# Another spacing for the first tile's rows, with the rows left out moved in two parts at the end

## The chip, the cores and the metric

The kernel runs on one core of one Trainium2 chip; nothing else runs beside it. The metric is the device time of one execution in microseconds (us). Lower is better.

## The reference

The kernel divides each row of 1024 values by the sum of the row's absolute values. There are 32 x 512 = 16,384 rows; 67.11 MB are read and as much is written.

```
x = np.random.randn(32, 512, 1024).astype(np.float32)
sums = np.sum(np.abs(x), axis=-1, keepdims=True)
return (x / (sums + 1e-8)).astype(np.float32)
```

## The kernel before

The tiles lie in SBUF, the core's working memory, in 128 partitions; each partition takes 128 of the 16,384 rows. The kernel moves them in eleven tiles: ten of 12 rows per partition (6 MB each) and a last one of 8. Within a tile a partition's rows lie together in DRAM, so neighbouring partitions of a 12-row tile start 12 x 4 KB = 48 KB apart. Loads are issued from the SP queue and stores from the ScalarE queue. Four tiles are in SBUF at a time. VectorE sums the absolute values and multiplies two thirds of the rows; ScalarE multiplies the other third.

```
    R = 12
    BUFS = 4
    per_partition = n // P
    ...
    rows = [R] * (per_partition // R)
    if per_partition % R:
        rows.append(per_partition % R)

    def piece(flat, i):
        a, k = P * sum(rows[:i]), rows[i]
        return flat[a : a + P * k, :].rearrange("(p r) d -> p r d", p=P)
    ...
    def normalize(x_tile, r0, k, kv):
        ...   # reduce of |x|, + EPS, reciprocal; VectorE multiplies kv rows, ScalarE the others

    with tc.manual_schedule():
        for i, k in enumerate(rows):
            x_tile = sbuf.tile([P, R, d], FP32)
            nc.sync.dma_start(out=x_tile[:, :k, :], in_=piece(x_flat, i))
            normalize(x_tile, 0, k, k - k // 3)
            nc.scalar.dma_start(out=piece(out_flat, i), in_=x_tile[:, :k, :])
```

## Time and profile before

| | before |
|---|---|
| time, median of the first 3 runs | 317.24 us (316.94 to 317.64) |
| span of the profiled run | 315.7 us |
| VectorE / ScalarE busy | 75% / 15% |
| DMA engines busy, by slices | 9 tenths in 38 of 40 slices |
| bytes moved, mean rate | 134.23 MB, 425 GB/s |

First some lines of the profile page of the kernel before. The line `DMA` gives the busy share of the 16 DMA engines in 40 equal slices, in tenths, and `GB/s` what they moved in each. The line of a group gives its busy time, the mean of one instruction in ns, and the idle time of the engine ahead of it. A line of the DMA issues ends with the KB of one transfer and the us from issue to landing.

```profile
span 315.7 us, 205 instructions
...
DVE 235.8 (75%) x44; ACT 46.1 (15%) x43; POOL 0.2 (0%) x4
...
DMA  8999999999999999999999999999999999999996
GB/s 318 467 405 436 455 380 423 405 473 423 399 479 417 405 479 411 423 461 411 455 436 405 473 417 405 473 423 399 486 406 411 479 413 421 438 455 411 455 401 274
DMA packets 3169, 134.23 MB, mean 425 GB/s; under 512 B 352, under 2 KB 352, under 8 KB 352
...
HBM read 67.11 MB, written 67.11 MB: 425 GB/s over the span
...
L45 DVE TENSOR_REDUCE s<-x_tile 128x12 f32<-128x12288 f32 (+1 forms) x11 | 138.2, 12562 | 58.0 <-DMA x_tile<-in_x_dram 58.0
...
x_tile<-in_x_dram SPq DMA_DIRECT2D x10, 6144.0 KB, 34.9
out_dram<-x_tile ACTq DMA_DIRECT2D x10, 6144.0 KB, 51.3
...
```

One line of the table of waits of the kernel before (total us, times, longest us):

```profile
...
DVE s L45 <- DMA x_tile<-in_x_dram: 58.0, 8, 18.6
...
```

And the timeline of the kernel before (start, length in us): the first reduce, then the end.

```profile
...
18.63 12.95 DVE L45 TENSOR_REDUCE s<-x_tile 128x12 f32<-128x12288 f32 x1 [18.63 <-DMA x_tile<-in_x_dram]
...
277.61 0.34 ACTq L74 DMA_DIRECT2D out_dram<-x_tile  x1
279.65 8.69 DVE L45 TENSOR_REDUCE s<-x_tile 128x8 f32<-128x8192 f32 x1 [2.13 <-DMA x_tile<-in_x_dram]
...
288.88 6.56 DVE L55 TENSOR_TENSOR x_tile<-x_tile,inv 128x6144 f32<-128x6144 f32 x1
295.53 0.34 ACTq L74 DMA_DIRECT2D out_dram<-x_tile  x1
```

The reader is to see two things. VectorE waits 58.0 us for loads, and its whole work of 235.8 us would fit under the transfers, so the DMA engines are the limit. And near the end VectorE is nowhere late enough to matter: the last store is issued at 295.53 us, while the DMA line is at 9 tenths until the last slice (a slice is 7.9 us).

The trace also records each single DMA packet with its queue, start, length and bytes. In this kernel one packet is one partition's part of a transfer: 49,152 bytes, or 32,768 in the last tile. The records don't name the engine. I joined each packet to the one whose end its start meets within 25 ns, which gives, in the kernel before, 16 chains of 8,388,608 bytes each, one for each engine, with hardly a gap. Two numbers from there carry the argument: the median 48 KB packet takes 1.815 us, and the one of 32 KB 1.213 us. Sixteen engines at 48 KB per 1.815 us are 433 GB/s. The Trainium skill, "DMA: Bandwidth & Descriptors", section "Where 436 GB/s comes from", puts the limit of the SBUF side at 435.2 GB/s; this trace agrees. So all but the edges of the run is at the ceiling.

Times from the packet records are counted from the start of the first packet, which is at 1.73 us on the clock of the timelines. Times with "issued" or "reduce" are from the timelines.

The lengths of the first packet of each of the 16 engines in load 0, from the same records, us, in order of their starts:

```
before  2.79 2.24 3.15 2.50 3.14 2.51 2.64 2.66 3.71 2.38 2.32 3.56 2.18 2.05 1.82 1.86
```

All but the last two are clearly longer than 1.815. This was the only visible slack at the start, and the change aims at it.

### The profile page before, as it was taken

To read this page: it belongs to the slowest core of one execution; us is meant where nothing else is said; L and a number is where in the kernel's file an instruction comes from. 1 tells how busy PE (TensorE), PEld (TensorE's weight loads), DVE (VectorE), ACT (ScalarE), POOL (GpSimd) and SP (SyncE) were. 2 spreads that over 40 slices of the span, in tenths; PEclk is the share of its full clock that TensorE was granted. 3 is DMA by queue.
4 is the path that set the end of the run, shared out by engine and by line. 5 is a ranking of instruction groups with operands and counts; after the bars stand their busy time and mean duration, and the time that the engine had idled before them with its cause. 6 is when DMAs were issued, how large, how long until landed. Compare 5 with 4: busy or idle time off the path is not lost.

```text
span 315.7 us, 205 instructions
## 1 busy us (share of the span) xinstructions
DVE 235.8 (75%) x44; ACT 46.1 (15%) x43; POOL 0.2 (0%) x4
## 2 busy tenths in 40 slices
DVE  0069999999999699739947991997399469979400
ACT  0010501303105003200500050032005000502000
POOL 0000000000000000000000000000000000000000
DMA  8999999999999999999999999999999999999996
GB/s 318 467 405 436 455 380 423 405 473 423 399 479 417 405 479 411 423 461 411 455 436 405 473 417 405 473 423 399 486 406 411 479 413 421 438 455 411 455 401 274
DMA packets 3169, 134.23 MB, mean 425 GB/s; under 512 B 352, under 2 KB 352, under 8 KB 352
## 3 DMA queue, kind: packets, MB, share of 16 engines
q1 hardware_dynamic: 1584, 67.11, 49.7%
q10 hardware_dynamic: 1584, 67.11, 49.1%
q14 instruction: 1, 0.01, 0.0%
HBM read 67.11 MB, written 67.11 MB: 425 GB/s over the span
## 4 chain that ended last, share of the span: by engine, by line
another core or an unknown queue 36%; DMA 31%; DVE 26%; SPq 0%; issue 0%; DVEq 0%; ACTq 0%
DMA x_tile<-in_x_dram 15%; DMA out_dram<-x_tile 15%; DVE s L45 15%; DVE x_tile L55 10%; SPq L72 0%; DVE inv L54 0%; DVE s L52 0%; DVEq L54 0%; ACTq L74 0%
## 5 line engine op out<-in xcount | busy, mean ns | idle before, releaser
L45 DVE TENSOR_REDUCE s<-x_tile 128x12 f32<-128x12288 f32 (+1 forms) x11 | 138.2, 12562 | 58.0 <-DMA x_tile<-in_x_dram 58.0
L55 DVE TENSOR_TENSOR x_tile<-x_tile,inv 128x8192 f32<-128x8192 f32 (+1 forms) x11 | 93.5, 8498 | 0.4
L62 ACT ACTIVATE x_tile<-x_tile,inv 128x1024 f32<-128x1024 f32 x42 | 44.9, 1137 | 226.3 <-DVE inv L54 226.3
L62 ACT ACT_TABLE_LOAD x1 | 1.3, 1283 | 18.7 <-DMA x_tile<-in_x_dram 18.7
L54 DVE RECIPROCAL inv<-s 128x12 f32<-128x12 f32 (+1 forms) x11 | 2.5, 225 | 0.9
L52 DVE TENSOR_SCALAR s<-s 128x12 f32<-128x12 f32 (+1 forms) x11 | 1.9, 173 | 0.4
L89 POOL MEMSET const-bfloat16-1.0<- 128x1 bf16 x1 | 0.1, 101 | 0.0
L89 POOL MEMSET const-uint8-127<- 128x1 uint8 x1 | 0.1, 101 | 0.0
L89 POOL MEMSET const-float32-0.0<- 128x1 f32 x1 | 0.1, 98 | 0.2 <-issue 0.2
L89 POOL MEMSET const-float32-1.0<- 128x1 f32 x1 | 0.1, 98 | 0.0
## 6 DMA issues: line engine op xcount, KB each, us to landing
x_tile<-in_x_dram SPq DMA_DIRECT2D x10, 6144.0 KB, 34.9
out_dram<-x_tile ACTq DMA_DIRECT2D x10, 6144.0 KB, 51.3
x_tile<-in_x_dram SPq DMA_DIRECT2D x1, 4096.0 KB, 30.4
out_dram<-x_tile ACTq DMA_DIRECT2D x1, 4096.0 KB, 19.1
```

Source lines behind the costliest of these rows:

```text
L45: nc.vector.tensor_reduce(out=s[:, :k], in_=x_tile[:, r0 : r0 + k, :], axis=mybir.AxisListType.X, op=mybir.AluOpType.add, apply_absolute_v ...
L52: nc.vector.tensor_scalar_add(out=s[:, :k], in0=s[:, :k], scalar1=EPS)
L54: nc.vector.reciprocal(out=inv[:, :k], in_=s[:, :k])
L55: nc.vector.tensor_mul(out=x_tile[:, r0 : r0 + kv, :], in0=x_tile[:, r0 : r0 + kv, :], in1=inv[:, :kv].unsqueeze(2).to_broadcast([P, kv, d]),)
L62: nc.scalar.activation(out=row, in_=row, func=mybir.ActivationFunctionType.Copy, scale=inv[:, r : r + 1],)
L89: nc = _bacc.Bacc("TRN2", target_bir_lowering=False, num_devices=1)
```

## The change

The intent, read from the diff: have the first tile's partitions start 64 KB apart in DRAM, by taking 12 of every 16 rows. The 4 rows that are left out of every 16 join the last tile. Since those and the 4 rows that remain at the end are not one region of DRAM, the last tile is loaded, normalized and stored in two parts of 4 rows.

```diff
-    rows = [R] * (per_partition // R)
-    if per_partition % R:
-        rows.append(per_partition % R)
+    FIRST = 16
+    rows = [R] * (per_partition // R) + [8]
 
-    def piece(flat, i):
-        a, k = P * sum(rows[:i]), rows[i]
-        return flat[a : a + P * k, :].rearrange("(p r) d -> p r d", p=P)
+    def block(flat, a, k):
+        return flat[P * a : P * (a + k), :].rearrange("(p r) d -> p r d", p=P)
+
+    def pieces(flat, i):
+        head = block(flat, 0, FIRST)
+        if i == 0:
+            return [(0, R, head[:, :R, :])]
+        a = FIRST + R * (i - 1)
+        if i < len(rows) - 1:
+            return [(0, R, block(flat, a, R))]
+        return [
+            (0, FIRST - R, head[:, R:, :]),
+            (FIRST - R, per_partition - a, block(flat, a, per_partition - a)),
+        ]
...
-            nc.sync.dma_start(out=x_tile[:, :k, :], in_=piece(x_flat, i))
-            normalize(x_tile, 0, k, k - k // 3)
-            nc.scalar.dma_start(out=piece(out_flat, i), in_=x_tile[:, :k, :])
+            for r0, m, src in pieces(x_flat, i):
+                nc.sync.dma_start(out=x_tile[:, r0 : r0 + m, :], in_=src)
+            for r0, m, dst in pieces(out_flat, i):
+                normalize(x_tile, r0, m, m - m // 3)
+                nc.scalar.dma_start(out=dst, in_=x_tile[:, r0 : r0 + m, :])
```

More of the change, by code (lines that the diff above doesn't have):

```diff
@@ L28 @@
     BUFS = 4
+    FIRST = 16
     per_partition = n // P
-    assert n % P == 0
-    rows = [R] * (per_partition // R)
-    if per_partition % R:
-        rows.append(per_partition % R)
-    def piece(flat, i):
-        a, k = P * sum(rows[:i]), rows[i]
-        return flat[a : a + P * k, :].rearrange("(p r) d -> p r d", p=P)
+    assert n % P == 0 and per_partition % R == 8
+    rows = [R] * (per_partition // R) + [8]
[12 more added lines that the diff above has]
+        ]
     sbuf = ctx.enter_context(tc.tile_pool(name="sbuf", bufs=BUFS))
@@ L69 @@
     with tc.manual_schedule():
-        for i, k in enumerate(rows):
+        for i in range(len(rows)):
             x_tile = sbuf.tile([P, R, d], FP32)
-            nc.sync.dma_start(out=x_tile[:, :k, :], in_=piece(x_flat, i))
-            normalize(x_tile, 0, k, k - k // 3)
-            nc.scalar.dma_start(out=piece(out_flat, i), in_=x_tile[:, :k, :])
+            for r0, m, src in pieces(x_flat, i):
[3 more added lines that the diff above has]
+                nc.scalar.dma_start(out=dst, in_=x_tile[:, r0 : r0 + m, :])
 _INS = ['x']
```

## The prediction

> **What bounds the kernel now.** DMA, from end to end. The page shows the DMA engines busy at 9 tenths in 38 of 40 slices, 134.23 MB at a mean of 425 GB/s. VectorE is busy 75%, ScalarE 15%; VectorE's largest wait (58.0 us in total, the table of waits) is for loads. The trace's single DMA packets say it more sharply: each of 128 partitions is one packet (48 KB, 32 KB in the last tile), 8 per DMA engine and transfer. The median 48 KB packet takes 1.815 us, the 32 KB one 1.213 us, so an engine's share is 2 x (80 x 1.815 + 8 x 1.213) = 309.8 us. From the first packet's start to the last one's end are 312.6 us. Only 2.8 us is not pure packet time on the engine that ends last.
>
> Where those 2.8 us are: the first packet of each engine takes 1.82 to 3.71 us, and two engines take 3.57 and 3.71. Nothing evens this out, as every engine has the same bytes: two engines, by their phase those two, end at 325.1 and 325.4 on the trace's clock, the others at 324.0 to 324.6. The slowest first packet sets the end.
>
> **What the change does.**
> 1. Start: the first tile's partitions begin 64 KB apart instead of 48 KB. Bytes and packets of load 0 stay; only which addresses the 16 engines hit together changes. If the slow pair becomes like the rest, about 1.0 us is gained; if power-of-two spacing makes more engines collide, 1 or 2 us are lost. The Trainium skill, "DMA: Bandwidth & Descriptors", section "Latency and other measured facts", reports 207 GB/s at a row pitch of 512 KiB against 214 padded, and large losses only from 2 MiB, so I expect no lasting slowdown at 64 KB; this trace has no such pitch to confirm it.
> 2. Tail: the last 8 rows per partition move as two parts of 4. VectorE's work is the same (8.69 + 6.56 us today, twice about 4.35 + 3.3 us after) plus one more set of small operations, 0.5 us. The 16 KB packets should take 0.61 us (from 1.815 and 1.213); 16 more packets per engine at 9 ns are 0.15 us.
> 3. Section "Queues, rings and completion order" of that page says that the engines alternate between queues packet by packet. 16 KB load packets then get a quarter of an engine beside 48 KB store packets, so the second part lands later: I estimate at 294 us, where today the last load's wait ends at 279.65. Its store is issued near 303 us instead of 295.5. But stores 7 to 9 and the first part's store advance by what the loads give up, and should keep the engines busy until about 308. The 4 to 5 us of slack should hide it.
>
> **On the critical path:** the first packets, wholly; of the tail only the 0.15 us.
>
> **Predicted:** 316.9 us, 8 in 10 between 315.8 and 318.6. Faster by over 2%: 0.01; within 2%: 0.96; slower by over 2%: 0.03. A gain of 2% (6.3 us) is ruled out by the 2.8 us above.
>
> **What would show it.** Step 1: the longest first packet of load 0, and the first reduce's start (18.63 us now); right if the end moves with the slowest first packet. Step 2: two 128x4096 reduces near 4.35 us. Step 3: the last reduce starting near 294 us and DMA still 9 tenths in every slice but the last.
>
> **What would make it wrong.** A wait between the parts that I don't foresee (part two's multiply waiting for part one's store, or a semaphore in use), idling the DMA engines by 5 to 10 us; step 3's slack being smaller; 64 KB spacing slowing all 8 packets of load 0.

## The result

| | before | after |
|---|---|---|
| median of 6 runs | 317.30 us (316.94 to 317.74) | 318.17 us (317.69 to 318.61) |
| span of the profiled run | 315.7 us | 316.8 us |
| ratio | | 1.0028, interval 1.0013 to 1.0043 |

A ratio here and below is the mean time of one kernel's fast runs over that of the other's in the same rounds, so not quite the ratio of the medians. The change costs 0.3%: the same within 2%, but measurably slower, where a small gain had been predicted.

The page of the changed kernel, the lines that answer to those of before:

```profile
span 316.8 us, 214 instructions
...
DVE 236.3 (75%) x48; ACT 46.3 (15%) x43; POOL 0.2 (0%) x4
...
DMA  8999999999999999999999999999999999999995
GB/s 323 472 397 478 416 366 428 403 484 403 441 453 397 459 434 397 478 416 416 478 397 459 434 397 465 428 410 484 397 448 447 397 459 420 389 447 472 397 411 250
DMA packets 3458, 134.24 MB, mean 424 GB/s; under 512 B 384, under 2 KB 384, under 8 KB 384
...
HBM read 67.11 MB, written 67.11 MB: 424 GB/s over the span
...
L58 DVE TENSOR_REDUCE s<-x_tile 128x12 f32<-128x12288 f32 (+1 forms) x12 | 138.3, 11527 | 63.6 <-DMA x_tile<-in_x_dram 63.6
...
x_tile<-in_x_dram SPq DMA_DIRECT2D x10, 6144.0 KB, 34.1
out_dram<-x_tile ACTq DMA_DIRECT2D x10, 6144.0 KB, 50.8
x_tile<-in_x_dram SPq DMA_DIRECT2D x2, 2048.0 KB, 34.1
...
```

The table of waits of the changed kernel, one line:

```profile
...
DVE s L58 <- DMA x_tile<-in_x_dram: 63.6, 8, 17.6
...
```

And its timeline, the first reduce and the end:

```profile
...
17.62 12.95 DVE L58 TENSOR_REDUCE s<-x_tile 128x12 f32<-128x12288 f32 x1 [17.62 <-DMA x_tile<-in_x_dram]
...
276.85 4.41 DVE L58 TENSOR_REDUCE s<-x_tile 128x4 f32<-128x4096 f32 x1
...
281.77 3.36 DVE L68 TENSOR_TENSOR x_tile<-x_tile,inv 128x3072 f32<-128x3072 f32 x1
...
285.22 0.34 ACTq L89 DMA_DIRECT2D out_dram<-x_tile  x1
293.40 4.42 DVE L58 TENSOR_REDUCE s<-x_tile 128x4 f32<-128x4096 f32 x1 [8.27 <-DMA x_tile<-in_x_dram]
...
298.75 3.36 DVE L68 TENSOR_TENSOR x_tile<-x_tile,inv 128x3072 f32<-128x3072 f32 x1
302.19 0.34 ACTq L89 DMA_DIRECT2D out_dram<-x_tile  x1
```

What to see: the first reduce starts at 17.62 us instead of 18.63, so load 0 was 1.0 us faster. The two small reduces are there (4.4 us each), the second part's data are waited for until 293.40 us, and its store is issued at 302.19 instead of 295.53. The DMA line is at 9 tenths up to the last slice all the same. So a microsecond was won at the start, no engine was left idle, and yet the end came a microsecond later. The page can't say more than that; the single packets can. (This profiled run took 318.61 us, the slowest of the six, so its trace shows the loss a little larger than the median does.)

First packets of load 0 in the changed kernel, us, in order of their starts:

```
after   2.51 2.60 2.62 2.53 2.39 2.58 2.60 2.45 2.55 2.51 2.65 2.48 2.47 2.25 2.47 2.22
```

The 3.71 and the 3.56 are gone. And the slow packets between 245 and 292 us after the first packet's start, all that took more than 60 ns over the usual length (start, length, kind; `store 48` is a 48 KB packet of a store):

```
before   271.003  1.467 load 32     271.353  1.366 load 32        (usual: 1.213)

after    258.005  1.996 store 48    258.025  2.024 store 48    258.057  2.020 store 48    258.108  1.880 store 48
         260.540  1.885 store 48    260.605  1.880 store 48    260.652  1.908 store 48    260.681  1.936 store 48
         265.466  2.456 store 48    265.519  2.531 store 48    265.554  2.565 store 48    265.625  2.598 store 48
         265.694  2.608 store 48
         285.469  2.007 store 48    285.596  2.021 store 48    285.666  2.074 store 48    285.769  2.111 store 48
         285.849  2.111 store 48                                   (usual: 1.815)
```

They lie on the same five chains, each of which loses 1.0 to 1.5 us there by the lengths of all its packets. Of the 16 engines the middle ones are done at 311.5 us after the first packet's start in both kernels; the last one is done at 312.61 in the kernel before and at 313.84 in the changed one. All engines have the same bytes, so nobody takes over what a slow one has left.

### The profile page after: what moved, and what is told of

Same layout as the page of the kernel before. It is cut to its first block, busy times and chain, and to the rows that moved or that the text cites. A ratio compares the mean times of both kernels' runs of the same rounds, so it can differ in the third digit from the quotient of the medians.

```text
span 316.8 us, 214 instructions
## 1 busy us (share of the span) xinstructions
DVE 236.3 (75%) x48; ACT 46.3 (15%) x43; POOL 0.2 (0%) x4
## 4 chain that ended last, share of the span: by engine, by line
another core or an unknown queue 36%; DMA 35%; DVE 23%; SPq 1%; issue 0%; DVEq 0%; ACTq 0%
DMA x_tile<-in_x_dram 19%; DMA out_dram<-x_tile 16%; DVE s L58 14%; DVE x_tile L68 9%; SPq L86 1%; DVE inv L67 0%; DVE s L65 0%; DVEq L67 0%; ACTq L89 0%
```

## The experiments

Twelve runs were made: eight new kernels, two of them twice, and the two known ones again. The theory after the result (T): the 64 KB start wins about 1 us, and the split tail loses about 2 us. The rivals: R1, the even start leaves the engines in step so that they collide later, and the tail is harmless; R2, the 64 KB spacing of the left-out rows slows the tail, not the split.

### The start alone (two runs of the same kernel)

```diff
-            nc.sync.dma_start(out=x_tile[:, :k, :], in_=piece(x_flat, i))
+            src = piece(x_flat, i)
+            if i == 0:
+                src = x_flat[: P * 16, :].rearrange("(p r) d -> p r d", p=P)[:, :R, :]
+            nc.sync.dma_start(out=x_tile[:, :k, :], in_=src)
```

> The kernel before with one thing changed: load 0 reads 12 of every 16 rows (64 KB apart), everything else as before; the result is wrong on purpose (some rows of tile 0 are others). Theory T (the start gains about 1 us by evening out the first packets; the split tail loses about 2 us again): slowest first packet near 2.6 us instead of 3.7, first reduce near 17.6 us instead of 18.6, all engines end within about 0.7 us of one another, time about 1 us under before (316.3). Rival R1 (the even start itself leaves the engines in step, and they collide later; the tail is harmless): first packets even as well, but slow packets at the first store and in the tail, ends spread over 2 us, time 0.5 to 1 us over before.

Measured: 317.35 us median of 5 runs against 317.26 for before; ratio 1.0000, interval 0.9988 to 1.0013. Its output is wrong, which doesn't matter for the time. The timeline shows the early first reduce:

```profile
...
17.71 12.95 DVE L45 TENSOR_REDUCE s<-x_tile 128x12 f32<-128x12288 f32 x1 [17.71 <-DMA x_tile<-in_x_dram]
...
```

The slowest first packet took 2.63 us, and in the profiled run all engines ended within 0.5 us of one another, with no slow packet in the tail. That run was the fastest of the five (316.58 us). In the mean nothing was gained. So the tail is innocent as long as it is whole, against R1; but T's gain of 1 us does not reach the end either. It was run again later:

> The start alone at 64 KB again (wrong result on purpose), for more times and a second trace. The cold starts showed 0.7 us less per load, so a load-by-load theory says 0.7 us under before (ratio 0.998). W (the end is set by the sum of all delays of the worst engine, and the gain at the first packet is partly paid back at the first store, which then hits all engines in step): ratio between 0.9985 and 1.000; engines' mean end 0.1 to 0.3 us under that of before's traces.

Measured: ratio 0.9999, interval 0.9982 to 1.0016, median 317.56 of 6 runs. Here three 32 KB packets of the last load took 1.9 to 2.0 us instead of 1.2, on three engines, and the last engine ended at 312.94 us after the first packet's start, 1.2 us after the mean. W's first half, the ratio, came as expected; its second, the engines' mean end, was 311.69 against 311.61 and 311.69 in the two traces of before: no gain there.

### The tail alone

The first tile is contiguous as before; the last tile's two parts are two contiguous blocks of 4 rows.

```diff
-        head = block(flat, 0, FIRST)
-        if i == 0:
-            return [(0, R, head[:, :R, :])]
-        a = FIRST + R * (i - 1)
+        a = R * i
...
-            (0, FIRST - R, head[:, R:, :]),
-            (FIRST - R, per_partition - a, block(flat, a, per_partition - a)),
+            (0, 4, block(flat, a, 4)),
+            (4, 4, block(flat, a + 4, 4)),
```

> First tile as before (48 KB apart), only the last 8 rows per partition in two parts of 4, both contiguous. Correct result. T: the tail alone costs about 2 us on some engines: time 1 to 2 us over before (318.3 to 319.3), slow store packets (2.0 to 2.6 us instead of 1.8) while 16 KB load packets run beside them. R1: 0.15 us over before (317.5), no such slow packets. Rival R2 (it is the 64 KB spacing of the left-out rows that slows the tail, not the split): 317.5 as well.

Measured: 318.30 us against 317.26; ratio 1.0034, interval 1.0022 to 1.0047; correct. Nine slow store packets (up to 2.52 us) between 245 and 292 us, and the last engine ends at 313.64. The four engines that hold these nine packets are the four that end last (312.81 to 313.64; all others by 311.99). This is the whole loss of the change, without its start and without its 64 KB spacing. R2 falls, and R1 with it. T's sign is right and its size is nearer to 1 us than to 2.

### Another spacing: 12 of every 20 rows

```diff
-    FIRST = 16
+    FIRST = 20
...
             (0, FIRST - R, head[:, R:, :]),
-            (FIRST - R, per_partition - a, block(flat, a, per_partition - a)),
```

With 80 KB between partitions the left-out rows are 8 per partition, which is the whole last tile, one load and one store.

> First tile takes 12 of every 20 rows (80 KB apart), the 8 rows it leaves out are the last tile, whole, one load and one store with 32 KB packets as before. Correct result. T, if any spacing other than 48 KB evens the start: 1 us under before (316.3). If 64 KB is special: slowest first packet 3 us or more, time within 0.3 us of before or above. R1: near before or 0.5 us above although the first packets are even.

Measured: 317.35 us against 317.26; ratio 1.0004, interval 0.9990 to 1.0018; correct. The slowest first packet took 2.94 us. So 64 KB is hardly special in this one trace, and again an even start gave no time. Five 32 KB packets of the last load were slow (up to 1.81 us instead of 1.21).

### The left-out rows in the second tile (two runs of the same kernel)

```diff
-        a = FIRST + R * (i - 1)
-        if i < len(rows) - 1:
-            return [(0, R, block(flat, a, R))]
-        return [
-            (0, FIRST - R, head[:, R:, :]),
-            (FIRST - R, per_partition - a, block(flat, a, per_partition - a)),
-        ]
+        if i == 1:
+            return [(0, 4, head[:, R:, :]), (4, 8, block(flat, FIRST, 8))]
+        a = R * i
+        return [(0, rows[i], block(flat, a, rows[i]))]
```

This keeps the 64 KB start and the whole last tile. The small load packets now run while no store is under way yet.

> 64 KB start as in the change, but the 4 rows that it leaves out join the second tile (4 + 8 rows in two parts) and the last tile is 8 rows in one part as before. Correct result. T: start gain kept and no split tail: 0.5 to 1 us under before (316.3 to 316.8), first reduce near 17.6 us. R1: ends spread as in the changed kernel, 0.5 to 1 us over before. R2: tile 1's loads have slow packets or its stores have.

Measured: 316.94 us against 317.26; ratio 0.9996, interval 0.9983 to 1.0008; correct. Again for a tighter interval:

> 64 KB start with the left-out rows in the second tile, again, for a tighter interval: within 0.3 us of before, below the changed kernel by about 1 us, no slow store packets between 245 and 292 us.

Measured: 316.94 us against 317.28; ratio 0.9986, interval 0.9970 to 1.0001. The medians are 0.34 us apart, just over the 0.3 expected. Both traces have a single slow store packet after 245 us (2.17 us), not none as expected. The loss of the change is gone in this arrangement: on the same chip, the changed kernel took 318.04 us. Whether it beats the kernel before is not shown: both intervals contain 1.

### Cold starts

Before the real loop, 24 loads into one buffer, each waiting for the one before; spacing 48 KB and 64 KB in turn.

```diff
     with tc.manual_schedule():
+        x_tile = sbuf.tile([P, R, d], FP32)
+        for i in range(24):
+            a, span = 8 * (i // 2), (12, 16)[i % 2]
+            src = x_flat[P * a : P * (a + span), :].rearrange("(p r) d -> p r d", p=P)
+            nc.sync.dma_start(out=x_tile, in_=src[:, :R, :])
+            t = stats.tile([P, R], FP32)
+            nc.vector.tensor_reduce(out=t[:, :1], in_=x_tile[:, :1, :], ...)
         for i, k in enumerate(rows):
```

> Before the real loop, 24 loads of 12 rows per partition into one buffer, each waiting for a small reduce of the one before, so that all DMA engines are idle at each start; even ones with partitions 48 KB apart, odd ones 64 KB apart. Correct result; the time is longer on purpose. S (the spacing evens out the first packets): the slowest first packet of the 12 starts at 64 KB has a mean at least 0.5 us below that of the 12 at 48 KB. D (it is a draw of each execution): the two distributions overlap, means within 0.3 us of each other.

Measured (761.09 us in all, one run), from the packet records, 12 loads each, mean and standard deviation:

```
                                       48 KB apart    64 KB apart
slowest first packet                   3.46 (0.15)    2.75 (0.10) us
mean of the 16 first packets           2.58 (0.06)    2.47 (0.06) us
first packet's start to last one's end 16.38 (0.11)   15.66 (0.08) us
```

S is right: the two spacings took turns within one execution, and the wider one evens out the first packets, and a load into idle engines is 0.72 us shorter. But the second row shows how that comes about: the mean engine gains only 0.11 us. The load ends when its last engine ends, so the load gains 0.7; the engines together gain little.

### Where the loss of the tail sits: stores split, or loads split

Both have the start of the kernel before. In the first the last 8 rows are loaded whole, then normalized and stored in two parts; in the second they are loaded in two parts, then normalized and stored whole. Against the kernel of the tail alone, the two parts are now the halves of the same 8 rows:

```diff
-            (0, 4, block(flat, a, 4)),
-            (4, 4, block(flat, a + 4, 4)),
+            (0, 4, block(flat, a, 8)[:, :4, :]),
+            (4, 4, block(flat, a, 8)[:, 4:, :]),
...  # the first kernel, loads whole:
-            for r0, m, src in pieces(x_flat, i):
+            for r0, m, src in [(0, rows[i], block(x_flat, R * i, rows[i]))]:
...  # the second kernel instead, stores whole:
-            for r0, m, dst in pieces(out_flat, i):
+            for r0, m, dst in [(0, rows[i], block(out_flat, R * i, rows[i]))]:
```

> 48 KB start as before; the last 8 rows are loaded whole (32 KB packets), normalized and stored in two parts of 4 rows. Correct result. If the small load packets are the cause of the tail's loss (L): within 0.3 us of before (317.3). If splitting the compute and the stores is (C): 1 us over before (318.3).

Measured: 317.39 us against 317.35; ratio 0.9998, interval 0.9984 to 1.0011; correct. No slow packet between 245 and 292 us. Its timeline: two reduces again, but the data of both are there at 279.22 us, as before.

```profile
...
279.22 4.42 DVE L55 TENSOR_REDUCE s<-x_tile 128x4 f32<-128x4096 f32 x1 [1.96 <-DMA x_tile<-in_x_dram]
...
287.43 4.41 DVE L55 TENSOR_REDUCE s<-x_tile 128x4 f32<-128x4096 f32 x1
...
296.24 0.34 ACTq L86 DMA_DIRECT2D out_dram<-x_tile  x1
```

> 48 KB start as before; the last 8 rows are loaded in two parts of 4 rows (16 KB packets), normalized and stored whole. Correct result. L: 1 us over before (318.3), with slow store packets (2.0 to 2.6 us) near the end of stores 7 and 8. C: within 0.3 us of before.

Measured: 324.01 us against 317.35; ratio 1.0205, interval 1.0191 to 1.0219; correct. There are 26 slow store packets (up to 2.45 us) between 245 and 292 us, so L holds for the packets. The time was missed by far, for a second reason, which its page and timeline show:

```profile
span 323.0 us, 207 instructions
...
DMA  8999999999999999999999999999999999999547
...
```

```profile
...
277.48 0.34 ACTq L86 DMA_DIRECT2D out_dram<-x_tile  x1
294.82 8.69 DVE L55 TENSOR_REDUCE s<-x_tile 128x8 f32<-128x8192 f32 x1 [17.43 <-DMA x_tile<-in_x_dram]
...
310.69 0.34 ACTq L86 DMA_DIRECT2D out_dram<-x_tile  x1
```

The last reduce waits until 294.82 us, and as it is now one of 8 rows, the store is issued only at 310.69. By then the earlier stores have run out: the packet chains of the engines have holes of 6.3 to 8.5 us, and the DMA line drops to 5, 4 and 7 tenths in the last slices. So splitting the load makes its end later, and only the split of the compute and the store, which the change also makes, keeps that off the end.

Why the load ends later is seen in the packets of one engine of the changed kernel, in order, from 250.2 us on (L load, S store, KB; 0 is the small packet that signals the end of a transfer):

```
S48 L0 S48 L16 S48 L16 S48 L16 S48 L16 S48 L16 S48 L16 S0 L16 S48 L16 S48 L0 S48 L16 S48 ...
```

A load packet and a store packet take turns. The Trainium skill, "DMA: Bandwidth & Descriptors", section "Queues, rings and completion order", says that each engine goes round the queues packet by packet, and the trace agrees. With packets of 16 KB against 48 KB a load gets a quarter of the engine.

### The kernel before, once more

> The kernel before, unchanged, for a second profile. S: again a pair of first packets at 3.5 to 3.7 us and the last engines 1 us behind the rest. D: another slowest first packet (between 2.6 and 3.7 us) on another engine, and the end moves with it.

Measured: one look, 317.06 us. The slowest first packet took 3.74 us, as S says, but the next took 3.04, so there was no pair. And that engine was not alone at the end: three ended within 0.06 us of one another, the last at 312.29 us after the first packet's start, and the next one at 311.90. The two beside it had first packets of 2.16 and 2.22 us which had started 1.1 to 1.2 us late. What the three have in common is that their first packets ended last of all, 3.33 to 3.77 us after the first start.

### The changed kernel, once more

> The changed kernel again, for a second trace beside the others: about 0.9 us over before (ratio 1.003); first packets even (slowest below 3 us), four to six engines with slow store packets in the tail, and the last engine at least 1 us behind the median one.

Measured: 318.04 us against 317.28; ratio 1.0021, interval 1.0004 to 1.0037. The slowest first packet took 2.92 us, and 28 store packets were slow (up to 2.82 us) between 245 and 292 us. Eight of them began within 1.1 us, so at least eight engines had one, not the four to six expected. This trace also has slow load packets at 112, 131, 141, 198 and 231 us, of which the first trace of the same kernel has a single one (at 229 us); they are unexplained, and they delay many engines at once. The last engine ended at 314.18 us, 1.0 us after the mean of all. The profiled run was the slowest of its six (318.83).

### Small load packets in the middle of the run

```diff
-            nc.sync.dma_start(out=x_tile[:, :k, :], in_=piece(x_flat, i))
+            src = piece(x_flat, i)
+            for r0, m in [(0, 4), (4, 8)] if i == 5 else [(0, k)]:
+                nc.sync.dma_start(out=x_tile[:, r0 : r0 + m, :], in_=src[:, r0 : r0 + m, :])
```

> The kernel before with only tile 5's load split into a part of 4 rows (16 KB packets) and one of 8 rows (32 KB), in the middle of the run; everything else as before, correct result. G (small load packets beside 48 KB store packets are slow anywhere): slow store packets (1.9 to 2.6 us) during tile 5's load on some engines, summing to at least 2 us over the engines, time 0.3 to 1 us over before. P (it belongs to the tail): no slow packets there, time within 0.3 us of before.

Measured: 339.35 us against 317.28; ratio 1.0686, interval 1.0663 to 1.0708; correct. Nobody expected that. Its page and the wait for tile 5:

```profile
span 336.8 us, 208 instructions
...
DMA  8999999999999999999999999999999999529747
...
```

```profile
...
155.25 12.95 DVE L45 TENSOR_REDUCE s<-x_tile 128x12 f32<-128x12288 f32 x1 [22.81 <-DMA x_tile<-in_x_dram]
...
```

During tile 5's load 23 store packets were slow, by 3.8 us in sum over the engines, so G is right there. But the load took 44 us (107.1 to 151.3), where tile 5's load takes 28 in the kernel before, as its packets of 16 and 32 KB take turns with store packets of 48 KB; VectorE waited 22.81 us for it, tile 5's store came late, and the later loads stayed late too (VectorE waits 11.13 us ahead of tile 9, against 6.78 in the kernel before). From 180 us on, 161 packets were slow although all but the last load's and store's were 48 KB again, and near the end most engines ran dry ahead of each of the last two stores, which were issued at 303.18 and 324.43 us (a DMA line of 5, 2, 9, 7, 4 and 7 tenths). So packets can be slow without small ones beside them. That the changed order of loads and stores slows them is the nearest reading, but it was not tried by itself.

### All traces side by side

From the packet records of one execution each; us, counted from the first packet's start. "Extra" is the sum over all engines of what packets took over 1.815, 1.213 or 0.611 us (48, 32, 16 KB).

| kernel | spacing | last load | slowest first packet | mean first packet | extra, 5 to 50 us | extra, 245 to 292 us | slow store packets there | mean end of the engines | last end |
|---|---|---|---|---|---|---|---|---|---|
| before | 48 | whole | 3.71 | 2.59 | 17.2 | 0.5 | 0 | 311.61 | 312.61 |
| before again | 48 | whole | 3.74 | 2.58 | 19.5 | 0.1 | 0 | 311.69 | 312.29 |
| stores split | 48 | whole | 3.13 | 2.53 | 17.5 | 0.1 | 0 | 311.74 | 312.23 |
| start alone | 64 | whole | 2.63 | 2.39 | 19.4 | 0.0 | 0 | 311.41 | 311.77 |
| start alone again | 64 | whole | 2.77 | 2.50 | 20.6 | 2.3 | 0 | 311.69 | 312.94 |
| second tile | 64 | whole | 2.90 | 2.48 | 20.7 | 0.4 | 1 | 311.69 | 312.16 |
| second tile again | 64 | whole | 2.89 | 2.46 | 19.2 | 0.4 | 1 | 311.64 | 312.15 |
| 80 KB | 80 | whole | 2.94 | 2.48 | 19.0 | 2.3 | 0 | 311.64 | 312.56 |
| tail alone | 48 | two parts | 3.17 | 2.54 | 18.2 | 4.1 | 9 | 311.91 | 313.64 |
| after | 64 | two parts | 2.65 | 2.49 | 21.0 | 6.3 | 18 | 312.07 | 313.84 |
| after again | 64 | two parts | 2.92 | 2.43 | 21.2 | 9.7 | 28 | 313.16 | 314.18 |
| loads split | 48 | two parts | 3.47 | 2.66 | 17.0 | 6.9 | 26 | 319.61 | 319.70 |
| middle | 48 | whole | 3.39 | 2.64 | 15.7 | not alike | not alike | 333.36 | 333.45 |

Two readings. First, the start. The six traces at 48 KB have a mean first packet of 2.59 us and the six at 64 KB one of 2.46, a gain of 0.13 us per engine. In the stretch from 5 to 50 us, in which the first store begins beside a load, those at 64 KB have 20.3 us of extra in the mean (19.2 to 21.2) and those at 48 KB 17.5 (15.7 to 19.5): (20.3 - 17.5) / 16 = 0.18 us per engine, paid back. The slow packets themselves, the load packets just ahead of the first store packets, show it: between 40.3 and 41.2 us, 16 load packets that take over 60 ns longer than usual begin in each of the six traces at 64 KB, as many as there are engines, and 11 to 14 in those at 48 KB, where the others come later. The first store's start shows the same: with the even start (64 and 80 KB) it is issued 38.1 to 38.4 us after the first packet's start, at 48 KB 38.6 to 39.1, yet its first packet runs at 43.3 to 43.6 us in all thirteen traces. The microsecond that load 0 was ahead is gone there; why this store doesn't begin earlier is not shown. Second, the tail. Small load packets at the end go with 9 to 28 slow store packets in all four traces that have them, and 0 or 1 in all eight that don't (the run "middle", whose order is another, is left out). Slow packets of a whole last load occur too, two to five in three of those eight; that is the 2.3 us of extra in "start alone again" and "80 KB".

## Why the prediction was right or wrong, point by point

The time, 318.17 us, lies in the stated range of 315.8 to 318.6, and "within 2%" was right. The direction was not: about 0.4 us less than before was predicted, 0.9 more came. That the time fell into the range is owed to the range's width of 2.8 us, not to the mechanism: the gain counted on didn't come, and a loss not counted on did.

- **"DMA, from end to end": right.** The change moved VectorE's last work by almost 7 us, and the DMA line stayed at 9 tenths. A gain of 2% was rightly ruled out.
- **Step 1, the first packets: right as far as load 0 goes.** The slowest went from 3.71 to 2.65 us, the first reduce from 18.63 to 17.62. The cold starts make it a property of the spacing: 3.46 against 2.75 us. "I expect no lasting slowdown at 64 KB" was right: after the first packet those of load 0 take 1.815 us again. The section "Latency and other measured facts", on which that rested, speaks of 512 KiB and more; nothing here contradicts it.
- **The step that failed: "The slowest first packet sets the end."** It was read from one trace, where it held. In the second trace of the same kernel the engine with the slowest first packet ended level with two others, whose first packets were short but began late. So a late start is visible at the end, but the end is set by the sum of all delays of the worst engine, of which the start is one: in "start alone again" three slow packets of the last load put it at 312.94 us. And the rest follow closely: without their late starters the two traces of before would still end at about 311.8 and 311.9 us instead of 312.6 and 312.3; by this estimate 0.4 to 0.8 us could be had, and not 1. The start alone, which takes 1 us off load 0, has ratios of 1.0000 and 0.9999. What the runs show in place of the step: the mean engine gains about 0.13 us at its first packet, pays about 0.18 at the first store, and ends where it did. The intervals still allow a gain of up to 0.4 us (0.12% of 317) by the first run and 0.6 us by the second. That the even start causes the dearer first store fits all traces, but was not tried by itself.
- **The second failure, a term of the sum that was mis-sized: step 2, "0.15 us" for the tail.** The extra packets were counted at their own cost only, and that was right: by the usual lengths an engine's packets add up to 309.95 us in the changed kernel and 309.81 before. What was left out is that other packets slow down. The tail alone measured 0.34%, 1.1 us of 317.2. The two that split one side each tell which half: splitting the stores costs nothing (0.9998); splitting the loads makes store packets of 48 KB take up to 2.45 us on some engines, and the engines with such packets are the ones that end last in the trace of the tail alone. The tail alone and the start alone make 1.0034 and 1.0000, together about what the change measured, 1.0028.
- **Step 3, the late second part: right in kind and size.** The last reduce starts at 293.40 us (294 said), its store is issued at 302.19 (303 said), and the first packets of that store run at 308.2 to 310.7, by engine (306.44 to 308.98 after the first packet's start at 1.73). A transfer into idle engines needs 1.0 us from issue to first packet, as load 0 shows (0.73 to 1.73), so about 5 us of slack were left on the earliest engine, where 4 to 5 had been estimated. The loads split alone shows what it costs where that slack is used up: 2%.
- **"What would make it wrong"** named idle DMA engines and a slow load 0. Neither came. Packets that take longer on a few engines were not on the list.

Why store packets become slow when small load packets take turns with them stays open. Time and place are shown (in the changed kernel stores 7 and 8, four or five engines almost at once), and the run with small packets in the middle has slow 48 KB packets without small ones beside them too. No experiment here separates the addresses from the order.

## What to carry to other kernels

When, as here, every DMA engine has its fixed share (8,388,608 bytes) and hardly a gap in it, count what a change does to the sum of an engine's delays, not how much earlier one transfer lands: a load that landed 1 us earlier gave nothing measurable at the end. Before you cut a transfer into smaller packets, look at what runs beside it: the queues took turns by packet here, so the smaller packets got the smaller share and landed later (44 us instead of 28), and in a pipeline with few buffers that can shift everything after it (22 us in the run with one load split in the middle). If rows must be left over, try them where only loads run: here, with them in the second tile, the loss was gone.

## What the Trainium skill lacked or had wrong

- "DMA: Bandwidth & Descriptors", "Latency and other measured facts", row pitch: it has nothing below 512 KiB and nothing about the first packet. Here 16 engines that start idle have a slowest first packet of 3.46 us at 48 KB and 2.75 us at 64 KB between partitions, and about 1.815 us for each later one at either.
- The same page, "Queues, rings and completion order", is right about turns by packet, but doesn't say what follows when the two queues' packets differ in size: a load of one 4-row and one 8-row part beside 48 KB store packets took 44 us instead of 28, and the kernel 339.35 us instead of 317.28.
- The same page, "SWDGE vs HWDGE vs iDMA", gives a packet as at most 4096 B preferably, in its table on what GpSimd builds, and no bytes for a transfer issued from SP or ScalarE. The packet records of such transfers here are 49,152 bytes, one per partition, and the turns between the queues are taken by these; whether a record is what the page calls a packet is not shown.
- No page has it that store packets stretch (1.815 to as much as 2.82 us) on some engines beside 16 KB load packets: the tail alone, which has them, is 0.34% slower.
